# Value heads as high and low halves of one stationary tile, with a new order of the first stage, the slots and the turns

## Chip, core and metric

The kernel runs on one core of a Trainium2 chip. A core has TensorE (PE, with its weight loads shown as PEld), VectorE (DVE), ScalarE (ACT), GpSimd (POOL) and SyncE (SP, which here issues the DMAs); they run side by side, each takes its own instructions in order, and they wait for one another by semaphores. The metric is the device time of one execution in microseconds (us).

## The reference

Two layers over 512 tokens of width 1024, all in float32. Each normalises its input, projects it into the inputs of four groups of heads, mixes, gates, projects back and adds:

```python
for l in range(DEPTH):
    h = _rmsnorm(x, norm_g[l])
    p = _split(h @ w_in[l])
    o_a = _mla(...)        # latent attention, 4 heads of 64
    o_b = _diff_attn(...)  # two softmax maps per head, then an RMSNorm per head
    o_c = _dsa(...)        # the top 128 keys of a query by an index score
    o_d = _short_conv(...) # gated convolution of width 3
    y = concatenate([o_a * silu(a_gate), o_b * silu(b_gate), o_c * silu(c_gate), o_d * silu(d_gate)])
    x = x + y @ w_out[l]
return _rmsnorm(x, final_g)
```

In each attention the probabilities p of a block of 128 queries are multiplied with the values v of a head (`einsum('bhqk,bkhd->bqhd', p, v)`); a query sees the keys of its own chunk of 64 and of those before it.

## The kernel before

**Precision.** A float32 operand is split into a high part, which ACT rounds to the format that TensorE reads (`fp32r`), and a low part, what is left, which DVE or POOL subtracts (`split_w` L104, `split_ps` L113). A product is three matmuls into one PSUM bank: high x high, high x low, low x high (`mm3` L122).

**Tiling.** Tokens are four blocks of 128. Features stand on the partitions for keys and queries, tokens for values. Attention runs by pairs of heads: `pair(k)` (L422) goes through two halves of the queries (256 each), two heads and the two blocks of 128 queries of a half. For each block a unit (`unit_a`, `unit_b`, `unit_c`) computes scores and probabilities. Then the block is turned (`flip`, L410: up to four 128x128 transposes on TensorE, split into the tiles `pth` and `ptl`), and when both blocks of a head are turned, `prod` (L440) multiplies with the values into the bank `ps_o`: per block of keys three matmuls of 256 columns, of 128 for the last one. The first half of the queries sees two key blocks (a short product, 6 matmuls), the second four (a long one, 12). The value tile `vt` of a pair is 192 wide: head 0 in columns 0 to 63, zeros, head 1 in columns 128 to 191 (`vtiles`, L378; POOL writes the zeros at L384). A stationary slice of 128 columns beginning at 64 j holds head j on its own rows of the result and zeros on the other head's, so both heads add up in one 128x256 region. `post_plain` (L470) and `post_b` (its `first` is at L779) read that region once and gate it.

**Order.** Program order gives priority; a scheduler emits the order of each engine from it. The engines in `START` keep the order of the code for the first stage of layer 0. That stage is the string `FIRST[0]` (L30): `l0` loads token block 0, `s` takes its sums of squares, `n` its norm, `w` loads a piece of the first weights, `c` splits it, `e0` transposes the normalised block, and `00` is the product of block 0 with piece 0; blocks with a complete row are followed by a small norm of the latents (`first_norm`, L521). Then come seven slots (`SLOTS`, L41): slot 0 the latent projections, slots 1 to 6 one pair each (two of a, of b, of c), and with them streams of other work, interleaved by `merge` in proportion to their planned cost: `qi`, `is` (index projection and scores), `ga` to `gc` (gates), `df`, `sp` (query and key projections of b and c), `tb`, `tc` (their values), `cv` (convolution). `TOP[i]` is the planned cost of the select rounds in slot i: 48 a layer, each a MAX8 and a MATCH_REPLACE8 on DVE (L594, L595); unit_c needs their result. A unit's turn, product and gating are queued `LAG` units later.

## Time and profile before

| | us |
|---|---|
| three timed runs, median (lowest to highest) | 679.08 (679.06 to 679.42) |
| the profiled execution | 679.76 |
| its span, first to last instruction | 678.0 |
| PE, PEld busy | 622.1, 533.6 |
| DVE, ACT, POOL busy | 487.4, 364.6, 278.5 |
| select rounds of layer 0, of layer 1 | 134.2 to 219.8, 453.3 to 538 |
| first unit_c of layer 0, of layer 1 | 251.0, 573.2 |

The busy shares are means over the span. The stretches have different limits, so they are read one by one, with the chain of work that ended last inside each and the list of what an engine waited for.

### The profile page before, as it was taken

The numbers are of one execution on the slowest core, as the hardware profiler recorded it, in microseconds if no ns is written. First come the engines' busy times: TensorE is split into PE (matmuls) and PEld (weight loads), VectorE is DVE, ScalarE is ACT, GpSimd is POOL, SyncE is SP. The second block draws the span as 40 slices with busy tenths as digits, with TensorE's granted clock in tenths as the row PEclk, the third lists the DMA queues.
The fourth block names the chain that finished last, engine by engine and source line by source line (L and its number), as shares of the span: only waits on it lengthen the run. The fifth ranks groups of instructions, "written<-read, shape, count | busy, mean of one in ns | idle before, by whom it ended". The sixth has DMA issues, their size and how long they took to land.

```text
span 678.0 us, 11037 instructions
## 1 busy us (share of the span) xinstructions
PE 622.1 (92%) x3599; PEld 533.6 (79%) x3607; DVE 487.4 (72%) x1441; ACT 364.6 (54%) x879; POOL 278.5 (41%) x408
## 2 busy tenths in 40 slices
PE   1999999789999898999989899999999999999994
PEld 1877787678789677899968687879878977789994
DVE  3767762599999796645395767779999959664536
ACT  6556583484552564554364566866545256355435
POOL 2375432315434343442431854242534344344255
PEclk9999999799999999999999999999999999999998
DMA  8446573763455411233253653457244641132203
GB/s 262 117 111 191 148 133 94 185 158 99 109 145 151 118 47 43 83 125 114 58 169 91 181 171 103 139 135 170 65 115 116 190 117 48 47 109 100 80 1 125
DMA packets 86697, 80.71 MB, mean 119 GB/s; under 512 B 7302, under 2 KB 73400, under 8 KB 86640
## 3 DMA queue, kind: packets, MB, share of 16 engines
q1 hardware_dynamic: 86640, 80.02, 42.4%
q8 instruction: 28, 0.46, 0.3%
q14 instruction: 29, 0.24, 0.1%
HBM read 65.22 MB, written 12.16 MB: 114 GB/s over the span
## 4 chain that ended last, share of the span: by engine, by line
PE 58%; DVE 26%; ACT 7%; DMA 5%; issue 2%; POOL 1%; SPq 0%; ACTq 0%; DVEq 0%; POOLq 0%
PE ps_proj L127 43%; PE ps_o L127 5%; DVE ia L595 5%; DVE m L594 4%; PE ps_pt L414 3%; PE ps_s L127 2%; DMA wr<-in_w_in_dram 2%; DVE ptl L116 2%; DVE big L119 1%; DVE ps_s L490 1%; ACT prob L478 1%; DMA big<-in_x_dram 1%; PE ps_pt L302 1%; ACT prob L482 1%; DVE ia L581 1%
## 5 line engine op out<-in xcount | busy, mean ns | idle before, releaser
L101 POOL TENSOR_TENSOR wl<-wr,wh 128x256 fp32r<-128x256 f32 (+1 forms) x304 | 226.8, 779 | 326.1 <-ACT wh L106 279.4
L127 PE MATMUL ps_proj<-big,wh 128*128 128x512 f32 x768 | 250.7, 401 | 2.1 <-DVE prob L472 1.0
L127 PE MATMUL ps_proj<-wh,big 128*128 128x256 f32 (+2 forms) x768 | 173.1, 310 | 4.6 <-DVE big L116 2.1
L127 PEld LDWEIGHTS ps_proj<-big,wh 128*128 128x128 f32 x768 | 138.8, 189 | 26.8 <-issue 1.5
L127 PE MATMUL ps_proj<-big,wl 128*128 128x512 f32 x384 | 151.7, 395 | 0.0
L127 PEld LDWEIGHTS ps_proj<-wh,big 128*128 128x128 f32 x768 | 129.9, 193 | 9.6 <-DVE big L116 2.6
L127 PE MATMUL ps_proj<-wl,big 128*128 128x256 f32 (+2 forms) x384 | 116.8, 304 | 0.0
L106 ACT CAST wh<-wr 128x1024 fp32r<-128x1024 f32 (+2 forms) x84 | 83.8, 999 | 43.2 <-PE ps_proj L127 20.6
L127 PEld LDWEIGHTS ps_proj<-big,wl 128*128 128x128 f32 x384 | 72.3, 188 | 14.2
L127 PEld LDWEIGHTS ps_proj<-wl,big 128*128 128x128 f32 x384 | 74.4, 194 | 2.0
L116 DVE TENSOR_TENSOR ptl<-ps_pt,pth 128x128 fp32r<-128x128 f32 (+1 forms) x96 | 46.5, 485 | 31.4 <-ACT pth L115 30.8
L127 PE MATMUL ps_o<-pth,vt 128*128 128x256 f32 (+1 forms) x288 | 60.0, 280 | 5.2 <-ACT pth L115 3.9
L115 ACT CAST pth<-ps_pt 128x128 fp32r<-128x128 f32 (+1 forms) x96 | 40.5, 425 | 44.0 <-PE ps_pt L414 43.6
L478 ACT ACTIVATE prob<-ps_s,st_a 128x128 f32<-128x128 f32 (+1 forms) x64 | 33.8, 529 | 47.8 <-DVE st_a L490 30.7
L127 PEld LDWEIGHTS ps_o<-pth,vt 128*128 128x128 f32 x288 | 49.1, 194 | 10.0 <-ACT pth L115 6.5
L414 PE MATMUL ps_pt<-ident,prob 128*128 128x128 f32 x240 | 43.2, 278 | 10.2 <-ACT prob L482 7.1
L595 DVE MATCH_REPLACE8 ia<-m,ia 128x256 f32<-128x256 f32 (+2 forms) x96 | 52.0, 544 | 0.2
L594 DVE MAX8 m<-ia 128x8 f32<-128x256 f32 (+2 forms) x96 | 50.9, 550 | 0.1
L127 PE MATMUL ps_o<-ptl,vt 128*128 128x256 f32 (+1 forms) x144 | 42.3, 294 | 4.7 <-DVE ptl L116 4.7
L414 PEld LDWEIGHTS ps_pt<-ident,prob 128*128 128x128 f32 x240 | 28.5, 140 | 22.3 <-ACT prob L482 12.5
L482 ACT ACTIVATE prob<-prob,st_a 128x128 f32<-128x128 f32 (+1 forms) x64 | 35.8, 564 | 9.5 <-DVE st_a L481 9.3
L581 DVE SCALAR_TENSOR_TENSOR ia<-prob,widx,ia 128x256 f32<-128x256 f32 (+2 forms) x42 | 26.2, 639 | 12.7 <-ACT prob L576 12.0
(160 smaller groups left out, 949.1 us busy)
## 6 DMA issues: line engine op xcount, KB each, us to landing
wr<-in_w_in_dram SPq DMA_DIRECT2D x56, 512.0 KB
big<-trip SPq DMA_DIRECT2D x64, 128.0 KB
trip<-big SPq DMA_DIRECT2D x28, 256.0 KB
big<-in_x_dram SPq DMA_DIRECT2D x7, 512.0 KB
wr<-in_w_in_dram SPq DMA_DIRECT2D x8, 416.0 KB
big<-trip SPq DMA_DIRECT2D x32, 96.0 KB
wr<-in_w_out_dram SPq DMA_DIRECT2D x8, 384.0 KB
big<-big SPq DMA_DIRECT2D x8, 256.0 KB
```

Source lines behind the costliest of these rows:

```text
L101: nc.gpsimd.tensor_tensor(out=o[:, c], in0=a[:, c], in1=b[:, c], op=OP.subtract)
L106: nc.scalar.copy(h[:, :n], raw[:, :n])
L115: nc.scalar.copy(hi, src)
L116: nc.vector.tensor_tensor(out=lo, in0=src, in1=f(hi), op=OP.subtract)
L119: nc.vector.scalar_tensor_tensor(out=lo, in0=src, scalar=scale, in1=f(hi), op0=OP.mult, op1=OP.subtract)
L127: nc.tensor.matmul(o, lhsT=a, rhs=b, start=start and i == 0 and j == 0, stop=stop and i == n - 1 and j == 2, skip_group_check=skip)
L414: nc.tensor.transpose(b[:, k * P:(k + 1) * P], p[:, k * P:(k + 1) * P], ident)
L478: nc.scalar.activation(p[:, :W], s[:, :W], AF.Exp, scale=-1.0, bias=mn, accum_out=sums)
L482: nc.scalar.activation(p[:, :W], p[:, :W], AF.Copy, scale=st[:, 2:3])
L581: nc.vector.scalar_tensor_tensor(out=a, in0=r[:, :W], scalar=w, in1=a, op0=OP.mult, op1=OP.add)
L594: nc.vector.max(out=m8, in_=a)
L595: nc.vector.match_replace(out=a, in_to_replace=m8, in_values=a, imm_value=MARK)
```

## The change

- **Values.** A value tile is 256 wide: for each head its 64 high columns and its 64 low columns, side by side. `prod` does two matmuls per key block, with `pth` and with `ptl` as moving operand, so each gives the high and the low part at once, on the two halves of the partitions; head j goes to columns 256 j of the bank. The zero memsets are gone.
- **Joining.** A new `joined` (L476 of the changed code) copies the low half of the result on ACT to a new tile `low` (one buffer) and adds it to the high half on DVE, head by head (64x256). `post_plain` and `post_b` call it first; in `post_b` two ACT passes over the bank become one over the joined tile, and the scale `subs` moves into the last step.
- **First stage.** A new order in `FIRST[0]`; ACT, DVE and PE keep the order of the code there, as SP did. The gain of the first norm is loaded as a row of 4 KB and spread over the partitions by two matmuls with a column of ones (`gain`), instead of a 512 KB broadcast by DMA; the first square root on ACT comes ahead of everything.
- **Slots and turns.** `SLOTS`, `TOP` and `PW` are set anew; a turn is queued one unit after its scores instead of two (`LAG`), with its first transpose, and the first matmul of a product, pinned behind what PE already has.

```diff
...
 EPS = 1e-6
 BIG = 1e30
 MARK = -3e38
-FIRST = ("l0 w0 l1 l2 w1 l3 w2 w3 s0 n0 s1 c0 e0 00 n1 s2 c1 e1 01 10 11 n2 s3 e2 c2 02 12 20 21 n3 e3 c3 03 13 22 23 30 31 32 33",
+FIRST = ("l0 w0 w1 l1 w2 w3 l2 l3 s0 g0 n0 c0 e0 c1 s1 00 10 n1 e1 c2 01 11 s2 n2 20 21 c3 e2 02 12 s3 n3 22 30 31 e3 32 03 13 23 33",
          "w0 w1 c0 c1 00 10 01 11 w2 w3 c2 c3 e2 20 30 02 12 21 31 e3 03 13 22 32 23 33")
 NBIG = 20
 PIECE = 256
...
 NPROB = 7
 NGATE = 3
 NPT = 2
-NVAL = 6
-TOP = (0,0,4,16,99,0,0)
-SLOTS = ('qi ga0 bl ga1', 'is|bi df0 gb0', 'sp1 tb', 'sp0 gc0 gb1 df1', 'tc cv0', 'cv1 gc1', '')
-PW = 9.0
+NVAL = 3
+TOP = (0, 0, 4, 10, 99, 0, 0)
+SLOTS = ('qi ga0 ga1|bl', 'bi df0 gb0|is gb1', 'sp1 tb', 'sp0 gc0|df1', 'tc cv0', 'cv1 gc1', '')
+PW = 10.0
 INORDER = set()
-START = {mybir.EngineType.SP}
+START = {mybir.EngineType.SP, mybir.EngineType.Activation, mybir.EngineType.DVE, mybir.EngineType.PE}
 FM = (456, 456)
 LATE = ((3, 3),)
 FW = (("wh", "wl"), WB)
-LAG = (2,3,4)
+LAG = (1, 3, 4)
 CH = (4.0,)
 BSTEP = 2
 PL = 13.0
...
     pv = sb("val", NVAL)
     pp = sb("prob", NPROB)
     pg = sb("gate", NGATE)
+    pl_pool = sb("low", 1)
     pt_pool = sb("ptr", NPT)
     pi = sb("idx", 1)
     sm = sb("small", 4)
...
         return y
 
 
+    one = const.tile([1, P], FT, name="one")
+    grow = const.tile([1, D], FT, name="grow")
+    warm = const.tile([1, 1], FT, name="warm")
     ident = const.tile([P, P], FT, name="ident")
     make_identity(nc, ident)
     identb = const.tile([P, P], BF, name="identb")
...
         for l in range(DEPTH):
             li = 0.8 - 0.6 * math.exp(-0.3 * l)
             nc.vector.tensor_scalar(out=subs[:, l:l + 1], in0=pcol[:, l * 10 + 3:l * 10 + 4],
-                                    scalar1=1.0 - li, scalar2=None, op0=OP.mult)
+                                    scalar1=0.5 * (1.0 - li), scalar2=None, op0=OP.mult)
             pr = sm.tile([P, 2, 32], FT, name="lpr", bufs=1)
             lv = lraw[:, l, :].rearrange("p (a c b) -> p a c b", a=2, c=2)
             nc.vector.tensor_tensor(out=pr, in0=lv[:, :, 0, :], in1=lv[:, :, 1, :], op=OP.mult)
...
 
         def vtiles():
 
-            vs = []
-            for _ in range(2):
-                vs.append([pv.tile([P, NT, 192], FR, name="vt", tag="vt") for _ in range(2)])
-                for v in vs[-1]:
-                    nc.gpsimd.memset(f(v)[:, :, 64:128], 0.0)
+            vs = [pv.tile([P, NT, 256], FR, name="vt", tag="vt") for _ in range(2)]
 
             def dst(t, src):
                 sv = src.rearrange("p (a h c) -> p a h c", a=2, h=2)
                 for a in range(2):
-                    hv, lv = (v[:, t, :].rearrange("p (h c) -> p h c", c=64)[:, 0::2, :] for v in vs[a])
-                    split_ps(hv, lv, sv[:, a])
+                    w = vs[a][:, t, :].rearrange("p (h c) -> p h c", c=64)
+                    split_ps(w[:, 0::2, :], w[:, 1::2, :], sv[:, a])
             return vs, dst
 
         def gate(c0):
...
             nb = qb + 1
             b = bank("pt")
             for k in range(nb):
-                nc.tensor.transpose(b[:, k * P:(k + 1) * P], p[:, k * P:(k + 1) * P], ident)
+                i = nc.tensor.transpose(b[:, k * P:(k + 1) * P], p[:, k * P:(k + 1) * P], ident)
+                if k == 0:
+                    tc.keep_in_program_order(i)
             c = (qb % 2) * P
             split_ps(pts[0][:, :nb, c:c + P], pts[1][:, :nb, c:c + P],
                      b[:, :nb * P].rearrange("p (k c) -> p k c", k=nb))
...
                                 if j == 0:
                                     box["o"] = bank("o")
                                 o = box["o"]
-                                pts = box[j]
+                                n = 0
                                 for kb in range(nb):
                                     c = P if kb == nb - 1 else 0
-                                    mm3(o[:, c:256], [tuple(x[:, kb, j * 64:j * 64 + P] for x in v)
-                                                      + tuple(x[:, kb, c:256] for x in pts)],
-                                        start=j == 0 and kb == 0, stop=j == 1 and kb == nb - 1, skip=True)
-                                return 0.33 * nb
+                                    for x in box[j]:
+                                        n += 1
+                                        i = nc.tensor.matmul(o[:, 256 * j + c:256 * j + 256], lhsT=v[:, kb, j * P:(j + 1) * P],
+                                                             rhs=x[:, kb, c:256], start=n == 1, stop=n == 2 * nb,
+                                                             skip_group_check=True)
+                                        if n == 1:
+                                            tc.keep_in_program_order(i)
+                                return 0.22 * nb
 
                             late.append((now + LAG[1], prod))
                             if j == 1:
...
             while late and (everything or late[0][0] <= clock[0]):
                 yield late.pop(0)[1]()
 
+        def joined(o, y):
+
+            low = pl_pool.tile([64, 512], FT, name="low")
+            nc.scalar.copy(low, o[64:P])
+            for j in range(2):
+                c = slice(256 * j, 256 * j + 256)
+                nc.vector.tensor_tensor(out=y[64 * j:64 * j + 64], in0=o[0:64, c], in1=low[:, c], op=OP.add)
+
         def post_plain(box, half, y, g):
             def part():
-                nc.vector.scalar_tensor_tensor(out=y, in0=box["o"][:, :256], scalar=0.5, in1=g,
-                                               op0=OP.mult, op1=OP.mult)
+                joined(box["o"], y)
+                nc.vector.scalar_tensor_tensor(out=y, in0=y, scalar=0.5, in1=g, op0=OP.mult, op1=OP.mult)
                 return 0
             return [part]
 
...
             e4 = ep4[half]
 
             def first():
-                o = box["o"][:, :256]
                 sq = box["sq"] = prob()
-                nc.scalar.activation(sq[:, :256], o, AF.Square)
-                nc.scalar.activation(y, o, AF.Copy, scale=subs[:, l:l + 1])
+                joined(box["o"], y)
+                nc.scalar.activation(sq[:, :256], y, AF.Square)
                 return 0
 
             def second():
...
                 for i in range(2):
                     nc.tensor.transpose(b[:, i * P:(i + 1) * P], sq[:, 256 + i * P:256 + (i + 1) * P], ident)
                 nc.vector.tensor_tensor(out=y, in0=y, in1=b[:, :256], op=OP.mult)
-                nc.vector.scalar_tensor_tensor(out=y, in0=y, scalar=0.5, in1=g, op0=OP.mult, op1=OP.mult)
+                nc.vector.scalar_tensor_tensor(out=y, in0=y, scalar=subs[:, l:l + 1], in1=g, op0=OP.mult, op1=OP.mult)
                 return 0.2
             return [first, second, third]
 
...
                     first_load(int(b))
                 elif a == "c":
                     first_split(int(b))
-                elif a in "lsne":
+                elif a in "lsneg":
                     enter(int(b), a)
                 else:
                     first_part(int(a), int(b))
...
         ctx.enter_context(tc.manual_schedule(engines=INORDER))
     h = Hidden()
     x0 = {}
-    g0 = raw_tile()
-
-    warm = sm.tile([P, 1], FT, name="warm", bufs=1)
-    nc.scalar.activation(warm, ident[:, 0:1], AF.Sqrt)
+    g0 = flat(big(FT))
+
+    def gain():
+
+        for n in range(2):
+            c = slice(n * 512, (n + 1) * 512)
+            b = bank("pt")
+            nc.tensor.matmul(b, lhsT=one, rhs=grow[:, c], start=True, stop=True)
+            nc.vector.tensor_copy(g0[:, c], b)
 
     def enter(t, what, h=h):
         if what == "e":
             h.fill(t, x0[t].xn)
+        elif what == "g":
+            gain()
         elif what == "n":
             x0[t].finish()
         elif what == "s":
...
             x0[t].part(slice(512, D))
         else:
             x = flat(big(FT))
+            if t == 0:
+                nc.sync.dma_start(grow, norm_g[0:1, :])
+                nc.vector.memset(one, 1.0)
+
+                nc.scalar.activation(warm, one[:, 0:1], AF.Sqrt)
             for n in range(2 if t == 0 else 1):
                 c = slice(n * 512, (n + 1) * 512) if t == 0 else slice(0, D)
                 nc.sync.dma_start(x[:, c], x_in[t * P:(t + 1) * P, c])
-            if t == 0:
-                load_g(norm_g[0], g0)
             x0[t] = Norm(x, g0)
 
     for l in range(DEPTH):
```

On PE, a long value product of the first two pairs (`ps_o` is the bank of the results, `vt` the values, `ps_s` scores, `ps_proj` projections, `ps_pt<-ident` a transpose). Before:

```order
L728 MATMUL ps_s<-big 128x512 x3
L573 MATMUL ps_s<-kst,big 128x384
L127 MATMUL ps_o<-pth,vt 128x256
L127 MATMUL ps_o<-ptl,vt 128x256
L127 MATMUL ps_o<-pth,vt 128x256 x2
L127 MATMUL ps_o<-ptl,vt 128x256
L127 MATMUL ps_o<-pth,vt 128x256 x2
L127 MATMUL ps_o<-ptl,vt 128x256
L127 MATMUL ps_o<-pth,vt 128x256
L127 MATMUL ps_o<-pth,vt 128x128
L127 MATMUL ps_o<-ptl,vt 128x128
L127 MATMUL ps_o<-pth,vt 128x128
```

After:

```order
L414 MATMUL ps_pt<-ident,prob 128x128 x3
L742 MATMUL ps_s<-big 128x128 x3
L452 MATMUL ps_o<-pth,vt 128x256
L452 MATMUL ps_o<-ptl,vt 128x256
L452 MATMUL ps_o<-pth,vt 128x256
L452 MATMUL ps_o<-ptl,vt 128x256
L452 MATMUL ps_o<-pth,vt 128x256
L452 MATMUL ps_o<-ptl,vt 128x256
L452 MATMUL ps_o<-pth,vt 128x128
L452 MATMUL ps_o<-ptl,vt 128x128
```

Twelve matmuls became eight, alternating between `pth` and `ptl`, and the second turn of the half now stands close ahead of its product.

On DVE, the gating of the first long result and what stands around it (`ia` are the index scores that the select rounds work on). Before:

```order
L581 SCALAR_TENSOR_TENSOR ia_871<-prob,widx,ia_871 128x384
L581 SCALAR_TENSOR_TENSOR ia_872<-prob,widx,ia_872 128x512 x2
L116 TENSOR_TENSOR ptl<-ps_pt,pth 128x4x128
L116 TENSOR_TENSOR big<-ps_proj,big 128x512
L472 SCALAR_TENSOR_TENSOR prob<-ps_o,gate 128x256
L116 TENSOR_TENSOR vt<-ps_proj,vt 128x2x64
L581 SCALAR_TENSOR_TENSOR ia_870<-prob,widx,ia_870 128x256
```

After:

```order
L608 MAX m_1488<-ia_906 128x8
L595 SCALAR_TENSOR_TENSOR ia_907<-prob,widx,ia_907 128x512
L482 TENSOR_TENSOR prob<-ps_o,low 64x256
L595 SCALAR_TENSOR_TENSOR ia_907<-prob,widx,ia_907 128x512
L482 TENSOR_TENSOR prob<-ps_o,low 64x256
L117 TENSOR_TENSOR ptl<-ps_pt,pth 128x3x128
L487 SCALAR_TENSOR_TENSOR prob<-prob,gate 128x256
```

The two additions of `joined` stand ahead of the gating, and the first select round (MAX) has come before it.

On DVE, the end of the first stage: the norm of the last token block, the splits of its transposes (`big<-ps_pt`), and the latent norms (`ssa`). Before:

```order
L116 TENSOR_TENSOR big<-ps_pt,big 128x2x128 x2
L286 SCALAR_TENSOR_TENSOR big<-big,nw,wr 128x512
L116 TENSOR_TENSOR big<-ps_pt,big 128x2x128 x4
L529 TENSOR_SCALAR ssa<-ssa 128x2
L532 RECIPROCAL ssa<-ssa 128x2
L533 TENSOR_TENSOR ssa<-ssa 128x2
L534 SCALAR_TENSOR_TENSOR ssa<-ssa 128x2
L535 SCALAR_TENSOR_TENSOR ssa<-ssa 128x2
L537 TENSOR_SCALAR big<-ps_proj,ssa 128x256
```

After:

```order
L549 SCALAR_TENSOR_TENSOR ssa<-ssa 128x2
L551 TENSOR_SCALAR big<-ps_proj,ssa 128x256
L551 TENSOR_SCALAR big<-ps_proj,ssa 128x128
L543 TENSOR_SCALAR ssa<-ssa 128x2
L546 RECIPROCAL ssa<-ssa 128x2
L547 TENSOR_TENSOR ssa<-ssa 128x2
L548 SCALAR_TENSOR_TENSOR ssa<-ssa 128x2
L549 SCALAR_TENSOR_TENSOR ssa<-ssa 128x2
L551 TENSOR_SCALAR big<-ps_proj,ssa 128x256
L551 TENSOR_SCALAR big<-ps_proj,ssa 128x128
L117 TENSOR_TENSOR big<-ps_pt,big 128x2x128 x4
```

The splits of the last block's transposes, which stood ahead of the first latent norm, now stand behind two of them (the second of these and the end of the first are shown).

## Rows read from the trace of the kernel before

**Rows 1.** The page: the span, busy times, and the chain's shares by engine.
```profile
span 678.0 us, 11037 instructions
...
PE 622.1 (92%) x3599; PEld 533.6 (79%) x3607; DVE 487.4 (72%) x1441; ACT 364.6 (54%) x879; POOL 278.5 (41%) x408
...
PE 58%; DVE 26%; ACT 7%; DMA 5%; issue 2%; POOL 1%; SPq 0%; ACTq 0%; DVEq 0%; POOLq 0%
```

**Rows 2.** Busy time of each engine by stretch (begin:end, length, then engines).
```profile
core 0: us, PE busy (x) PEld busy (x) DVE busy (x) ACT busy (x) POOL busy (x), PEclk, DMA share, GB/s
41.00:134.20 93.20, 85.42 (x433) 70.67 (x433) 58.00 (x136) 52.17 (x122) 38.54 (x56) 0.96 0.59 148
134.20:219.80 85.60, 79.96 (x480) 68.99 (x479) 84.55 (x279) 45.64 (x112) 32.38 (x50) 1.00 0.52 135
219.80:251.00 31.20, 28.03 (x144) 22.09 (x143) 26.48 (x98) 16.89 (x47) 12.85 (x18) 1.00 0.31 86
251.00:349.00 98.00, 94.33 (x629) 84.49 (x631) 56.33 (x170) 49.89 (x112) 37.67 (x55) 1.00 0.27 90
...
453.30:538.00 84.70, 82.56 (x513) 72.78 (x512) 84.05 (x280) 45.44 (x113) 33.01 (x51) 1.00 0.50 129
538.00:573.00 35.00, 33.66 (x170) 26.84 (x170) 26.04 (x98) 18.15 (x49) 18.25 (x26) 1.00 0.33 88
```

**Rows 3.** The chain (start, length, work), at 58 us and around 300 us.
```profile
58.63 17.84 PE ps_proj L127 x83
...
294.61 1.37 PE ps_o L127 x12
295.97 3.28 PE ps_proj L127 x27
...
303.37 0.65 PE ps_o L127 x6
```

**Rows 4.** What PE waited for: total us, times, longest.
```profile
PE ps_pt L302 <- DVE big L286: 13.8, 1, 13.8
PE ps_pt L414 <- ACT prob L482: 7.1, 10, 1.5
PE ps_o L127 <- DVE ptl L116: 4.7, 5, 1.5
PE ps_o L127 <- ACT pth L115: 3.9, 5, 1.7
```

**Rows 5.** Groups of instructions by form: busy us, mean ns of one, idle before them.
```profile
L490 DVE CUSTOM_DVE_ANT_0 ps_s<-ps_s,bias,m 128x256 f32<-128x256 f32 x48 | 23.0, 487 | 0.5
...
L116 DVE TENSOR_TENSOR ptl<-ps_pt,pth 128x512 fp32r<-128x512 f32 x24 | 16.4, 684 | 7.3 <-ACT pth L115 7.3
...
L116 DVE TENSOR_TENSOR big<-ps_pt,big 128x256 fp32r<-128x256 f32 x32 | 12.8, 417 | 5.9 <-ACT big L115 5.6
...
L115 ACT CAST big<-ps_proj 64x512 fp32r<-64x512 f32 x16 | 9.2, 581 | 3.4 <-DVE big L116 2.1 <-PE ps_proj L127 1.1
...
L384 POOL MEMSET vt<- 128x256 f32 x24 | 6.7, 313 | 23.6 <-PE ps_o L127 23.6
...
L472 DVE SCALAR_TENSOR_TENSOR prob<-ps_o,gate 128x256 f32<-128x256 f32 x16 | 6.7, 416 | 9.4 <-PE ps_o L127 8.7 <-POOL big L101 0.7
```

**Rows 6.** DVE in order of time (start, length, work): the first block's norm factor.
```profile
7.17 0.16 DVE L283 SCALAR_TENSOR_TENSOR nw<-nw 128x1 f32<-128x1 f32 x1
```

**Rows 7.** The chain of the first 45 us, up to the latent norms.
```profile
3.09 7.95 DMA big<-in_x_dram
...
12.94 0.76 DVE big L286
13.84 1.09 PE ps_pt L302 x4
...
37.36 0.74 ACT prob L527 x4
...
41.11 0.75 DVE big L537 x2
```

## Prediction

> **What bounds the kernel now.** I read the page first [rows 1]. Over the span TensorE (PE) is busy 622.1 us of 678.0 and holds 58% of the chain that ended last; VectorE (DVE) is busy 487.4 us but holds 26% of it, so somewhere DVE is the limit. The table by stretch [rows 2] says where. While the 48 select rounds of a layer run (134.2 to 219.8, and 453.3 to 538 in the second layer), DVE works 84.55 of 85.60 us and 84.05 of 84.70. From 41.00 to 134.20 and from 219.80 on, PE is the fuller engine (85.42 of 93.20; 94.33 of 98.00) and DVE has a third or so to spare. So a microsecond of PE work is worth a microsecond outside the select windows and little inside, and DVE work the other way round.
>
> The chain in a PE stretch gives the pace of a matmul better than the busy time of one, since matmuls overlap [rows 3]: 27 projections of 256 columns take 3.28 us (0.121 each), 83 of 512 columns 17.84 us (0.215 each), a long value product (12 matmuls) 1.37 us, a short one (6) 0.65 us.
>
> Last I read what PE waits for [rows 4]: 13.8 us for its first operand, then 7.1 us before transposes of the probabilities (the "turns") and 4.7 + 3.9 us inside products, for the split of the turned block on ACT and DVE.
>
> The run of the profile took 679.76 us, 1.76 over its span and 0.68 over the median, 679.08. The sum is made against 679.76; the difference to the median is far below its uncertainty.
>
> **Value products.** Each layer has 12 long and 12 short ones. With the values' high and low halves side by side in one stationary tile, a key block needs two matmuls instead of three: 432 become 288. A third of 24 x 1.37 + 24 x 0.65 goes: 11.0 + 5.2 = **16.2 us of PE**. All of it counts where PE is the limit; inside the select windows it leaves PE idle.
>
> TensorE's price first by the row: 12 matmuls, nine of 256 and three of 128 columns, in 1.37 us. The Trainium skill ("TensorE: Matmul & The Clock Gate", Back-to-back issue gap) gives N/2.4 + 2.5 ns for an isolated matmul; an estimate by that page is 9 x 0.109 + 3 x 0.056 = 1.15 us for the same product, and 13 us saved instead of 16.2. The row is the dearer one and I stay with it.
>
> What comes in their place is on ACT and DVE. Each of the 24 results is now two halves on different partitions. `joined` copies one on ACT (64x512, nearest row 581 ns) and adds it on DVE in two pieces of 64x256 from PSUM (nearest row: 128x256, 417 ns) [rows 5]: 24 x 0.58 = 14 us of ACT, and 48 x 0.417 = **20 us of DVE** at most. Sixteen of the 24 had a DVE pass on that bank before too (416 ns) [rows 5], which now reads SBUF instead. On ACT nothing stands still for 14 us: in its fullest window it works 52.17 of 93.20 [rows 2]. On DVE the price depends on the place: by the order of the changed program 12 of a layer's 24 adds lie between its first and last select round, 12 x 0.417 = 5.0 us there; the rest falls where DVE has room. The bank of the results is held some 1.2 us longer (copy and adds against one pass); the next product into it comes several score blocks later, so I cost this at nothing, and at 24 x 1.2 = 29 us if nothing covered it. The copy waits on ACT for the product, with the exponentials of the next blocks queued behind it and the turns of those behind these; as it is queued one unit after its product (LAG 3 and 4), PE's work of a unit covers it. The 24 POOL memsets of the value tiles (313 ns, after long waits for PE [rows 5]) go; POOL is at 41% [rows 1], so they were worth nothing.
>
> **Order of the slots.** I counted instructions between markers in both orders. In layer 0, from the first stage to the first select round, 27 matmuls of 512 columns and 49 of 256 leave: 27 x 0.215 + 49 x 0.121 = 11.7 us, with the 128-column ones about 13.8. Into the select window come 46 of 512 and 31 of 256: 9.9 + 3.8 = 13.7, with the rest 15.3; between it and the first unit_c 27 and 11 leave, 7.1, with the rest 9. Layer 1 is alike: 45 of 512 enter the window, 53 leave the stretch behind it. So projections and attention units move into the windows. With them DVE work goes in: 235 instructions become 290 in layer 0's window (12 adds, 16 of the biased minimum at 487 ns [rows 5], 9 splits of the kind of 684 ns or less [rows 5], the rest small). Summed by their mean durations that is 103.6 to 122.2 us; the durations overlap (103.6 stands for 84.55 busy [rows 2]), so the window grows by 18.6 x 84.55/103.6 = 15.2 us, and in layer 1 by 15.2 x 84.05/104.8 = 12.2.
>
> Stage by stage, then: before the window of layer 0, -13.8 of PE and about -3 of its waits, -16.8; window +15.1; behind it -6.7 (between -9.2 by PE and nothing); unit_c and output -1. Layer 1: -5, +12.2, -10.5, -0.7. Moving work thus gives nearly nothing by itself; what is left is the third of the products.
>
> **First stage.** Now PE starts at 13.84. The factor of the first block's norm is ready at 7.33 [rows 6]; it is applied only at 12.94, since in DVE's order a weight split and the second block's sums stand ahead of it, and these wait for the second block of x until 11.04 [rows 7]. After the change the first block's gain needs a 4 KB row and two matmuls instead of a 512 KB broadcast, and the order is written out, so the first transposes can start at 7 to 8.5: 5 to 6 us earlier. But the order of ACT, DVE and PE is now fixed, and each PE step waits in turn for the eviction ahead of it. The largest such wait I find: the splits of the last block's transposes stand behind two whole latent norms on DVE. Such a norm took 37.36 to 41.86 here, with ACT in between [rows 7]; I count 3.7 us for PE there and 5 to 6 in smaller waits. Net -0.3, between -5 (none of these waits bites) and +2.
>
> **Turns and products.** LAG turns a block one unit after its scores instead of two, and pins a turn's first transpose and a product's first matmul behind what PE has. If the block isn't ready, all of PE stands. Measured on the order as PE work between scores and turn, and against the time that a block takes to be ready in the trace, the shortfall over all turns and products is 16.2 us after and 16.6 before. I take no change; the ends are -10 (half of the waits go) and +20.
>
> **Sum.** By stages -0.3 - 16.8 + 15.1 - 6.7 - 1 - 5 + 12.2 - 10.5 - 0.7 = -13.7. By PE alone -16.2. I take the middle, -14.8: 679.8 - 14.8 = **665.0 us**.
>
> **Rivals.**
> - A, more is gained. The first stage gives its 5 us and half of PE's waits around turns and products goes as well, since turns spread evenly: 15.7 us in rows of over 3 us, some 20 with the small entries [rows 4], so 10, of which the sum has 3 already: 665 - 5 - 7 = 653. For it: PE's first wait is 13.8 us [rows 4]; against: the fixed order of e3 behind two norms.
> - B, DVE eats half. The windows are full [rows 2], and what enters them, joins included, is paid at the full durations: 18.6 + 15.2 instead of 27.3 costs 6.5 more, so 671 to 674. The joins' 48 small adds cost 20 us by the row [rows 5], of which 10 lie in windows. The Trainium skill ("VectorE: DVE Perf Modes", Rules for kernel authors) says to keep the number of operations low, because each one drains the pipeline; that speaks against two adds where one of 512 columns would do. By the rows the second add costs 2 x 417 - 684 = 0.15 us a join, under 4 us in all.
> - C, slower. The pinned turns make PE stand: of the 48 turns and the products that follow at a short distance about 35 get a wait like the longest shown, 1.5 us, where now ten turns wait 7.1 us and ten times in products 8.6 [rows 4]. 35 x 1.5 = 52 against 16: 36 - 15 = +21, 700; it decides from 15 us of added waits, 10 turns more at full price, and with half of it the time is 683.
> - D, the change doesn't do what it says: the two matmuls cost as three did, for instance because the second waits for the low half. Then only DVE's added work shows: 680 to 685. Against it: the low half was the second operand before too, and it waited 4.7 us in all.
>
> **How the numbers follow.** Forecast (658 to 669) 0.47, A 0.23, B 0.20, C 0.07, D 0.03. A itself spreads from 648 to 657, B from 669 to 676. The range, 652 to 674, leaves out a third of A, a quarter of B and nearly all of C and D: about 0.2. 0.2% is about what a measurement here can tell from no change. Faster: all of the first three and little else, 0.88; same 0.03 (between B and D); slower 0.09.
>
> **What would show it.** Right: ps_o matmuls x288 and PE busy about 16 to 20 us lower; select windows of about 100 and 97 us, DVE full in them; the stretches ahead of and behind them shorter by 17 and 7, and by 5 and 10; the first transposes at 7 to 9 us and the first stage's end near 41. A: end near 36, and waits for turns under 4 us. B: windows over 104 us. C: waits of transposes on prob above 20 us. The forecast is wrong if PE's idle time grows by more than it does in the windows, or if the windows don't grow at all.

## The result, and the profile after

The changed kernel takes 656.86 us (median of four runs, 654.86 to 658.69) against 679.25: a ratio of 0.9667, 95% interval 0.9642 to 0.9693, or 22.4 us less. The forecast was 665.0, range 652 to 674. The profiled execution is the longest of the four (658.69, span 656.9, mean granted clock 0.982 where the others have 0.987 to 0.990), so its sums show 21 of the 22.4 us.

The page of the changed kernel, the lines that answer to [rows 1]:

```profile
span 656.9 us, 10797 instructions
...
PE 616.1 (94%) x3461; PEld 518.9 (79%) x3467; DVE 502.2 (76%) x1492; ACT 378.0 (58%) x894; POOL 270.0 (41%) x384
```

PE is busy 6 us less, not 16. Of the 10 us between, 3.8 are the gain's matmuls, which begin at 2.39 us; in the stretches below PE is busy 9.8 us less (622.1 to 612.3), with some 5 us more of them at the lower clock. The rest of the way to 16 is not accounted for. DVE and ACT each gained some 14 us of work. Busy time by stretch, cut at the same events as [rows 2] (first transposes, end of the first stage, first and last select round, first unit_c, layer 1, and the same again). The bounds here are the first MAX and the end of the last MATCH_REPLACE to the hundredth; by them the select windows before were 132.21 to 220.47 and 450.85 to 538.85, about 3 us longer than in [rows 2]:

```profile
core 0: us, PE busy (x) PEld busy (x) DVE busy (x) ACT busy (x) POOL busy (x), PEclk, DMA share, GB/s
8.52:38.51 29.99, 27.23 (x129) 21.90 (x129) 22.23 (x66) 18.56 (x56) 9.16 (x12) 1.00 0.44 134
38.51:114.63 76.12, 69.69 (x324) 56.05 (x325) 52.51 (x106) 44.77 (x101) 35.78 (x52) 0.96 0.66 164
114.63:221.58 106.95, 102.39 (x585) 86.36 (x584) 102.49 (x340) 61.50 (x153) 39.67 (x58) 0.97 0.53 136
221.58:240.61 19.03, 18.54 (x95) 14.88 (x94) 17.86 (x65) 11.52 (x26) 8.23 (x12) 1.00 0.21 61
...
431.53:534.38 102.85, 98.82 (x588) 83.88 (x587) 100.98 (x335) 60.62 (x149) 42.80 (x61) 1.00 0.51 129
534.38:553.67 19.29, 18.69 (x95) 14.91 (x94) 18.29 (x67) 11.80 (x27) 8.26 (x12) 1.00 0.24 69
```

In the windows PE and DVE are now both full (102.39 and 102.49 of 106.95). The stretches behind them, 31 and 34 us before, are 19. Cut at the same events in both profiles:

| stretch | before | after | difference | forecast |
|---|---|---|---|---|
| to the first transposes, and first stage | 41.04 | 38.51 | -2.5 | -0.3 |
| layer 0, to the first select round | 91.17 | 76.12 | -15.1 | -16.8 |
| its select window | 88.26 | 106.95 | +18.7 | +15.1 |
| to the first unit_c | 30.56 | 19.03 | -11.5 | -6.7 |
| unit_c and output | 97.93 | 95.93 | -2.0 | -1.0 |
| layer 1, to the first select round | 101.89 | 94.99 | -6.9 | -5.0 |
| its select window | 88.00 | 102.85 | +14.9 | +12.2 |
| to unit_c | 34.30 | 19.29 | -15.0 | -10.5 |
| to PE's end | 96.00 | 94.44 | -1.6 | -0.7 |

What PE waited for, as in [rows 4], the entries of 0.8 us and more at turns and products:

```profile
PE ps_pt L414 <- ACT prob L496: 5.2, 11, 1.0
PE ps_pt L414 <- DVE prob L784: 4.1, 10, 0.9
...
PE ps_o L452 <- DVE prob L482: 0.9, 2, 0.7
PE ps_pt L414 <- ACT prob L590: 0.9, 2, 0.7
PE ps_o L452 <- ACT pth L116: 0.8, 3, 0.4
```

Products, which waited 8.6 us for their turned blocks and 9.9 in all, wait 1.7 in all, of which 0.9 is for the bank `ps_o` that the joining still reads (L482). Turns wait about as long as before (10.4 for 9.9 with the small entries). And the chain through products, as in [rows 3]:

```profile
587.81 0.89 PE ps_o L452 x8
...
602.63 0.41 PE ps_o L452 x4
```

A long product takes 0.89 us instead of 1.37, a short one 0.41 instead of 0.65. Summed over all products in both traces, from the first matmul's start to the start of what follows, 53.5 us became 36.2.

### The profile page after: what moved, and what is told of

The parts are those of the page before. It is cut to its first block, busy times and chain, and to the rows that moved or that the text cites. A ratio compares the mean times of both kernels' runs of the same rounds, so it can differ in the third digit from the quotient of the medians.

```text
span 656.9 us, 10797 instructions
## 1 busy us (share of the span) xinstructions
PE 616.1 (94%) x3461; PEld 518.9 (79%) x3467; DVE 502.2 (76%) x1492; ACT 378.0 (58%) x894; POOL 270.0 (41%) x384
## 5 line engine op out<-in xcount | busy, mean ns | idle before, releaser
L102 POOL TENSOR_TENSOR wl<-wr,wh 128x256 fp32r<-128x256 f32 (+1 forms) x304 | 224.2, 770 | 314.4 <-ACT wh L107 226.7
L128 PE MATMUL ps_proj<-wh,big 128*128 128x256 f32 (+2 forms) x768 | 170.0, 307 | 4.2 <-DVE big L117 3.1
L128 PEld LDWEIGHTS ps_proj<-big,wh 128*128 128x128 f32 x768 | 141.3, 191 | 26.0 <-DVE big L120 1.4
L128 PEld LDWEIGHTS ps_proj<-wh,big 128*128 128x128 f32 x768 | 128.2, 192 | 9.2 <-DVE big L117 2.3
L128 PEld LDWEIGHTS ps_proj<-big,wl 128*128 128x128 f32 x384 | 72.8, 190 | 14.2
L492 ACT ACTIVATE prob<-ps_s,st_a 128x128 f32<-128x128 f32 (+1 forms) x64 | 33.7, 527 | 39.3 <-DVE st_a L744 19.6
L414 PE MATMUL ps_pt<-ident,prob 128*128 128x128 f32 x240 | 45.3, 288 | 11.5 <-ACT prob L496 5.2
L102 POOL TENSOR_TENSOR big<-prob,big 128x256 fp32r<-128x256 f32 x32 | 23.8, 764 | 35.9 <-ACT big L405 29.3
L452 PE MATMUL ps_o<-pth,vt 128*128 128x256 f32 (+1 forms) x144 | 35.9, 273 | 1.9 <-DVE prob L482 0.9
L452 PE MATMUL ps_o<-ptl,vt 128*128 128x256 f32 (+1 forms) x144 | 34.7, 288 | 0.0
L595 DVE SCALAR_TENSOR_TENSOR ia<-prob,widx,ia 128x256 f32<-128x256 f32 (+2 forms) x42 | 28.4, 690 | 6.8 <-ACT prob L590 5.6
```

What stands on the lines that cost most here:

```text
L102: nc.gpsimd.tensor_tensor(out=o[:, c], in0=a[:, c], in1=b[:, c], op=OP.subtract)
L128: nc.tensor.matmul(o, lhsT=a, rhs=b, start=start and i == 0 and j == 0, stop=stop and i == n - 1 and j == 2, skip_group_check=skip)
L414: i = nc.tensor.transpose(b[:, k * P:(k + 1) * P], p[:, k * P:(k + 1) * P], ident)
L452: i = nc.tensor.matmul(o[:, 256 * j + c:256 * j + 256], lhsT=v[:, kb, j * P:(j + 1) * P], rhs=x[:, kb, c:256], start=n == 1, stop=n == 2 * nb,
L492: nc.scalar.activation(p[:, :W], s[:, :W], AF.Exp, scale=-1.0, bias=mn, accum_out=sums)
L595: nc.vector.scalar_tensor_tensor(out=a, in0=r[:, :W], scalar=w, in1=a, op0=OP.mult, op1=OP.add)
```

## Experiments

An edit of this code lets the scheduler set the whole order anew, so each run gives the price of an edit with the order that follows from it. For two quantities I use sums over the ten stretches from the first transposes on: PE idle (length less PE busy), and time at the lower clock (two times one less PEclk, times the length, since the low level is half of the high one). Both come from the one profiled execution of a kernel.

**The parts by themselves.** First the products alone, in the kernel before:

```diff
-                vs.append([pv.tile([P, NT, 192], FR, name="vt", tag="vt") for _ in range(2)])
+            vs = [pv.tile([P, NT, 256], FR, name="vt", tag="vt") for _ in range(2)]
...
-                                    mm3(o[:, c:256], [tuple(x[:, kb, j * 64:j * 64 + P] for x in v)
+                                    for x in box[j]:
...
+        def joined(o, y):
```

> The kernel before with the new value products alone (value tiles of 256, two matmuls per key block, the joining on ACT and DVE, no pins); first stage, slots and turns as they were. If the third of the value products that goes from TensorE is what gained, and the 48 additions are nearly free: 679.3 - 16 = 663 (661 to 666). If the additions eat a good part of it inside the select windows, which stay as they were: 668 to 672, with the windows about 5 us longer each. If the products brought nothing by themselves and the order of the slots did it: 677 or more.

Measured: 685.92, ratio to the kernel before 1.0083 (1.0052 to 1.0115). Slower, as in the third case: neither 16 us gained nor 10.

Then all but the products, that is the changed kernel with the old ones (the diff above reversed):

> The changed kernel with the old value products (three matmuls per key block, zero halves, no joining); first stage, slots, lags as changed, turns' first transposes pinned. If the products gained 16 us and the joining is free: 656.9 + 16 = 673 (670 to 675). If the joining costs about 10 us in the select windows (12 additions of 0.417 us in each, and the copies): 663 to 667, since its cost goes too. If the order alone made the gain: 657 to 660.

Measured: 674.93, ratio 0.9915 (0.9884 to 0.9946). The new order with the old products gains 4.9 us over the runs of before taken with it (679.83), and the products in the new order 18. In the old order they lose 6.1 against the same runs. The 18 hold one thing more: in this kernel the turns' first transposes are pinned, but not the first matmul of a product; what that pin is worth alone was not run.

**The slots.**

```diff
-TOP = (0, 0, 4, 10, 99, 0, 0)
-SLOTS = ('qi ga0 ga1|bl', 'bi df0 gb0|is gb1', 'sp1 tb', 'sp0 gc0|df1', 'tc cv0', 'cv1 gc1', '')
-PW = 10.0
+TOP = (0,0,4,16,99,0,0)
+SLOTS = ('qi ga0 bl ga1', 'is|bi df0 gb0', 'sp1 tb', 'sp0 gc0 gb1 df1', 'tc cv0', 'cv1 gc1', '')
+PW = 9.0
```

> The changed kernel with SLOTS, TOP and PW of before. By my stage table the moving of work into the windows is worth little by itself: 656.9 + 2 (655 to 661), the select windows back to about 90 us and the stretches behind them to about 26 to 31. If the order is what gained, because it takes away the idle time of TensorE behind the windows and the waits of the stretch before them: 664 or more.

Measured: 691.77, ratio 1.0159 (1.0131 to 1.0186): 35 us over the changed kernel, and slower than before. That is far above the first case and inside the second, which had no upper end. With `TOP` as changed and only the streams and PW old:

> The changed kernel with the old SLOTS and PW alone, TOP as changed; the kernel with all three old took 691.8. If the streams of the slots, by which the index scores end and the select rounds begin 19 us earlier, are the cause: 686 to 693. If the share of the select rounds in slot 3 (TOP) is the cause: 657 to 662.

Measured: 693.30, ratio 1.0182 (1.0142 to 1.0221), at the upper end of the first case. It is the streams (with PW), not the share of the select rounds.

Where does the time go? In the products-alone kernel PE is busy 82.85 of 95.23 us in the first select window, at a granted clock of 0.93, and the stretch behind it runs at 0.86:

```profile
133.72:228.95 95.23, 82.85 (x470) 71.13 (x469) 91.00 (x292) 49.28 (x118) 34.57 (x50) 0.93 0.52 130
228.95:264.57 35.62, 29.42 (x132) 23.20 (x131) 26.20 (x98) 16.61 (x47) 10.81 (x16) 0.86 0.24 67
```

One stall in it is 8.10 us long. Its place in three timelines, PE, DVE and ACT:

```profile
179.70 1.22 PE L128 MATMUL ps_proj<-big,wh 128*128 128x512 f32 x2 [8.10 <-ACT prob L485]
```

```profile
174.12 1.16 DVE L601 MAX8 m<-ia 128x8 f32<-128x384 f32 x2
...
178.08 0.68 DVE L601 MAX8 m<-ia 128x8 f32<-128x512 f32 x1
178.79 0.30 DVE L497 CUSTOM_DVE_ANT_0 ps_s<-ps_s,bias 128x128 f32<-128x128 f32 x1
```

```profile
179.19 0.37 ACT L485 ACTIVATE prob<-ps_s,st_b 128x128 f32<-128x128 f32 x1 [6.32 <-DVE st_b L497]
```

PE's scores of a block (`ps_s`) were done at 171.6. The biased minimum that the block needs next, L497, stands in DVE's order behind select rounds and comes at 178.79; ACT's exponential waits for it, and PE for that. Nothing else had been put ahead on PE. The clock falls during the stall, by stretches of 5 us:

```profile
165.00:170.00 5.00, 4.88 (x23) 3.71 (x22) 4.90 (x14) 3.48 (x8) 5.00 (x7) 1.00 0.42 112
170.00:175.00 5.00, 1.49 (x9) 0.87 (x7) 4.84 (x11) 1.16 (x2) 2.82 (x5) 0.99 0.85 235
175.00:180.00 5.00, 0.30 (x1) 0.30 (x2) 4.97 (x19) 0.81 (x5) 0.00 (x0) 0.50 0.11 24
180.00:185.00 5.00, 5.00 (x14) 3.83 (x14) 4.13 (x17) 2.13 (x6) 2.81 (x4) 0.50 0.02 3
185.00:190.00 5.00, 5.00 (x24) 4.18 (x23) 4.13 (x16) 2.35 (x7) 0.00 (x0) 0.98 0.94 203
```

PE, full again from 180 on, issues 14 matmuls in 5 us at 0.50 where it issues 24 in the next 5. The four kernels with new products in old streams all have this stall, of 7.95 to 8.60 us, at 168 to 175 us; those with the new streams, or with the old products, have none above 3.9 from the first transposes on. Why the old products in the old streams escape it is not shown.

| kernel | us, median | us, profiled | PE busy | PE idle | at the lower clock |
|---|---|---|---|---|---|
| before | 679.25 | 679.76 | 622.1 | 33.2 | 10.6 |
| products alone | 685.92 | 685.22 | 613.0 | 46.8 | 33.9 |
| changed, slots old | 691.77 | 690.31 | 619.8 | 51.4 | 38.0 |
| changed | 656.86 | 658.69 | 612.3 | 27.3 | 15.8 |

Between the last two the profiled executions differ by 31.6 us (the medians by 34.9): 24.1 us of idle time and 7.5 more of busy time for the same work. The 22.2 us more at the lower clock can make up to half of themselves, 11.1, of busy time; PE stood idle in part of them.

**One stream.** The index scores (`is`) must end before the select rounds begin. In the new streams the gate projection gb1 is chained behind them, which doubles the planned cost of that stream, so that `merge` runs the scores in the first half of the slot; and gb1 no longer stands in slot 4. This one move in the products-alone kernel:

```diff
-SLOTS = ('qi ga0 bl ga1', 'is|bi df0 gb0', 'sp1 tb', 'sp0 gc0 gb1 df1', 'tc cv0', 'cv1 gc1', '')
+SLOTS = ('qi ga0 bl ga1', 'is gb1|bi df0 gb0', 'sp1 tb', 'sp0 gc0 df1', 'tc cv0', 'cv1 gc1', '')
```

> The kernel before with the new value products (values_only, 685.9) and one move of a stream: the gate projection gb1 goes from slot 4, inside the select window, into the stream of the index scores in slot 1, so that the scores end in the first half of that slot and the select rounds can begin earlier. Everything else is as before. If the begin of the select rounds is what the streams changed: the first MAX near 115 to 120, and 665 to 672. If it takes the other streams, the pins or the first stage as well: 680 or more.

Measured: 662.68, ratio 0.9747 (0.9730 to 0.9764), below the better case. From 685.92: 23 us for one name in a string, and 17 under the kernel before. The window, again with the stretch behind it:

```profile
119.86:215.13 95.27, 92.06 (x557) 80.56 (x556) 94.09 (x304) 54.33 (x129) 38.87 (x56) 1.00 0.55 146
215.13:248.20 33.07, 29.45 (x143) 23.57 (x142) 29.06 (x103) 17.48 (x48) 11.96 (x16) 0.95 0.23 68
```

It is as long as in the products-alone kernel (95.27 and 95.23) and DVE is about as full, but it holds 557 matmuls instead of 470, begins 14 us earlier, and PE keeps its clock in it. Over the whole kernel PE is idle 31.0 us and 9.7 us at the lower clock. The move does two things at once, it lets the select rounds begin earlier and takes gb1 out of slot 4, and no run separates them. And the same move undone in the changed kernel:

```diff
-SLOTS = ('qi ga0 ga1|bl', 'bi df0 gb0|is gb1', 'sp1 tb', 'sp0 gc0|df1', 'tc cv0', 'cv1 gc1', '')
+SLOTS = ('qi ga0 ga1|bl', 'bi df0 gb0|is', 'sp1 tb', 'sp0 gc0|df1 gb1', 'tc cv0', 'cv1 gc1', '')
```

> The changed kernel with that one move undone: the index scores alone in their stream, gb1 behind df1 in slot 4. If the begin of the select rounds decides: the first MAX near 133, TensorE idle some 20 us more and longer at the low clock, 680 to 693. If the move is a small part of the new streams: 657 to 664.

Measured: 673.52, ratio 0.9930 (0.9903 to 0.9957): 16.7 us worse, idle 39.3, lower clock 20.6; the first MAX comes at 125.76. That lies between the two cases that I had written down, and about half of what the old streams cost in all (36 us); which of the other streams, or PW, holds the rest was not tried.

**The joining.** The additions left out, in the products-alone kernel and in the changed one (the low part of the values is missing from the output):

```diff
-            low = pl_pool.tile([64, 512], FT, name="low")
-            nc.scalar.copy(low, o[64:P])
             for j in range(2):
                 c = slice(256 * j, 256 * j + 256)
-                nc.vector.tensor_tensor(out=y[64 * j:64 * j + 64], in0=o[0:64, c], in1=low[:, c], op=OP.add)
+                nc.scalar.copy(y[64 * j:64 * j + 64], o[0:64, c])
```

> The kernel with the new value products alone, and in it the joining without its additions: ACT copies the high half of each head's result and the low half is left out, so the output lacks the low part of the values. Takes 48 additions, about 20 us, from DVE, and leaves TensorE's work and the order of the slots as in values_only (685.9). If the additions in the full select windows are what ate the products' gain: 665 to 670, the windows back to 88. If the loss comes from the old slots and from where the scheduler puts the select rounds, whatever the additions cost: 680 or more.

Measured: 684.27, ratio 1.0050 (1.0026 to 1.0075), with the same long stall (7.95 us). The additions are not what ate the gain in the old order.

> The changed kernel with the joining without its additions in the same way (the low part of the values is left out). Its select windows are full on DVE (102.5 of 107 us) and hold about half of the 48 additions. If DVE sets the windows: 10 us less, 647 (644 to 650). If TensorE, which works 102.4 of 107 us in them too, is as much the bound: 653 to 656.

Measured: 653.92, ratio 0.9610 (0.9574 to 0.9645) against 0.9667 for the changed kernel: about 3 us for 48 additions of this size, with ACT's copies 3.3 us dearer than in the changed kernel (48 of 361 ns for 24 of 583):

```profile
L482 DVE TENSOR_TENSOR prob<-ps_o,low 64x256 f32<-64x256 f32 x48 | 19.9, 414 | 6.2 <-ACT low L479 5.7
...
L479 ACT COPY low<-ps_o 64x512 f32<-64x512 f32 x24 | 14.0, 583 | 5.6 <-PE ps_o L452 5.1
```

The first window without them is 12.6 us shorter (94.32), the stretch behind it 7.3 longer (26.30): work of PE that the window no longer covers comes out behind it.

**Turns.**

```diff
-LAG = (1, 3, 4)
+LAG = (2, 3, 4)
```

> The changed kernel with turns two units after their scores instead of one, still pinned. By the shortfalls on the order nothing changes: 656.9 (654 to 659). If turning early was worth its place, because products then find their blocks ready: 661 or more. If turning early makes TensorE wait for probabilities (9.3 us of such waits in the profile): 650 to 653.

Measured: 656.83, ratio 0.9655 (0.9618 to 0.9693). No difference in time, though the turns' waits are nearly gone, 2.2 us for 10.4. One entry of them is left above 0.8 us:

```profile
PE ps_pt L414 <- DVE prob L784: 1.6, 2, 1.2
```

PE's idle time over the stretches is 30.8 us, against 27.3: what the turns no longer wait for, other work waits for. Without the pins:

```diff
-                if k == 0:
-                    tc.keep_in_program_order(i)
...
-                                        if n == 1:
-                                            tc.keep_in_program_order(i)
```

> The changed kernel without pins on the turns' first transpose and the products' first matmul. Turns wait 9.3 us in all in the changed kernel. If the pins hold TensorE up: 650 to 654. If they are what makes products find their blocks ready (1.9 us of waits before products now, 8.6 before): 660 to 668. If neither: 656 to 658.

Measured: 665.65, ratio 0.9792 (0.9776 to 0.9808): the pins are worth 8.8 us. Its waits at the same places:

```profile
PE ps_pt L414 <- DVE prob L780: 6.6, 15, 1.1
PE ps_pt L414 <- ACT prob L492: 4.6, 11, 1.2
...
PE ps_o L450 <- DVE ptl L117: 2.7, 4, 0.9
```

Here products wait for `ptl` again, and turns too wait somewhat longer. These entries are only 2 to 4 us more; PE's idle time is 33.3 us instead of 27.3, so without the pins PE also waits elsewhere. Of the 6 us, 2.6 lie ahead of the first select window and 1.4 ahead of the second; which waits they are is not shown.

**The first stage.**

```diff
-FIRST = ("l0 w0 w1 l1 w2 w3 l2 l3 s0 g0 n0 c0 e0 c1 s1 00 10 n1 e1 ...
+FIRST = ("l0 w0 l1 l2 w1 l3 w2 w3 s0 n0 s1 c0 e0 00 n1 s2 c1 e1 01 ...
...
-START = {mybir.EngineType.SP, mybir.EngineType.Activation, mybir.EngineType.DVE, mybir.EngineType.PE}
+START = {mybir.EngineType.SP}
...
-    g0 = flat(big(FT))
+    g0 = raw_tile()
```

> The changed kernel with the first stage of before (its order, the broadcast of the gain by DMA, only SP's order fixed). In the profiles the first stage ended at 41.04 before and 38.51 after: +2.5, so 659.4 (657 to 662), with the first transposes at 13.8 and the stage's end at 41. A rival: the earlier start is taken back by the next wait (the weights' DMA or the latent norms), so that no difference is left: 656 to 658.

Measured: 658.61 (657.46 to 662.03), ratio 0.9681 (0.9646 to 0.9717), which the intervals don't tell from the changed kernel. In its profile the stage ends at 41.22 against 38.51, 2.7 us later; the timed medians differ by 1.75, the profiled executions by 0.6, so how much of it reaches the time is open. In the changed kernel PE's start and its wait at the last block's transposes:

```profile
8.52 2.16 PE L306 MATMUL ps_pt<-ident,big 128*128 128x128 f32 x8 [2.38 <-DVE big L290]
...
32.07 0.47 PE L128 MATMUL ps_s<-wh,big 128*128 128x456 f32 x1 [0.26 <-ACT big L116]
...
33.69 0.68 PE L128 MATMUL ps_s<-wh,big 128*128 128x456 f32 x2 [0.95 <-DVE big L117]
```

**A version meant to be better.** It moves the plain gating to POOL (the factor 0.5 goes into the joining, not shown) and takes the last block's transposes ahead of the second latent norm:

```diff
-                nc.vector.scalar_tensor_tensor(out=y, in0=y, scalar=0.5, in1=g, op0=OP.mult, op1=OP.mult)
+                nc.gpsimd.tensor_tensor(out=y, in0=y, in1=g, op=OP.mult)
...
-s3 n3 22 30 31 e3 32
+s3 n3 22 30 e3 31 32
```

> A version meant to beat both: the gating of the 16 plain results goes from DVE to POOL (the factor 0.5 into the joining), and the last block's transposes in the first stage go ahead of the second latent norm. Takes 16 x 0.416 = 6.7 us from DVE, of which about half in the windows, and some 1 us of waits from the first stage; without the 48 additions (20 us of DVE) the time fell by 2.9, so 0.5 to 1 us for this part by the same ratio: 655.3 (654 to 656.5). If POOL's slower pass delays what waits for the gated results: 657 to 659.

Measured: 657.84 (654.85 to 659.32), ratio 0.9672 (0.9650 to 0.9694): the same as the changed kernel. The first stage does end 1.8 us earlier (36.74), and the first window is 4.1 shorter (102.85 for 106.95), but the stretch behind it is 2.3 longer, and in layer 1 the stretch ahead of the window and unit_c are longer by 1.4 and 2.4. The changed kernel's own runs spread over 3.8 us, so what is left of such a gain can't be seen.

## Why the prediction was right, point by point

- **Value products, -16.2 us of PE: the size was right.** By the chain a long product went from 1.37 to 0.89 and a short one from 0.65 to 0.41: 24 x (0.48 + 0.24) = 17.3, and the sum over all products fell by the same 17.3. Inside products a matmul of 256 columns takes 120 ns from start to start at the median in both traces and one of 128 about 61. An estimate by the formula of the Trainium skill for an isolated matmul ("TensorE: Matmul & The Clock Gate", Back-to-back issue gap) is 109 and 56 ns; the rows decide, and they are the dearer ones. PE's busy time was the wrong sign to look for: it fell by 6 us on the page, where I had put 16 to 20, and by 14.2 in the stretches against the kernel with the old products in the new order (626.5).
- **"All of it counts where PE is the limit": right in the new order, wrong as a statement on the products.** In the old streams the same products made the kernel 6.1 us slower. The step that I missed is that work taken from PE must leave PE something to do while DVE sits in select rounds. In the changed kernel it does (102.39 of 106.95).
- **"Moving work gives nearly nothing by itself": right by itself, and the wrong question.** With old products the whole new order gains 4.9 us. With new ones the streams and PW decide over 36 us, 17 to 23 of them through one projection; with it moved, the select rounds begin earlier. I priced the move as work times pace and had no term for PE standing, nor for the lower clock that comes with it: between the old slots and the new 24 us of idle time and 7.5 of busy time.
- **The stages.** Seven of nine came within 3.6 us, and all signs are right. The mis-sized terms are the stretches behind the windows (-26.5 for -17.2): I took them between PE's work and nothing, and they followed PE's work (27.39 to 18.54 us busy in the first) and lost their idle time too (3.2 to 0.5 us). The windows grew by 33.5 for 27.3, the first with 6.4 us at the lower clock in it, so these two errors, -9.3 and +6.2 us, partly cancel, which is luck.
- **Joining, up to 20 us of DVE.** Duration right (414 ns for 417, 583 for 581); the price is 3 us, since PE is nearly as full in the windows, and its work comes out behind them. So rival B, DVE eating half, fell by its price, though one of its signs came: the first window is over 104 us (106.95), the second is not (102.85). The bank held longer, which I cost at nothing, made products wait 0.9 us. Whether one addition a join would be cheaper than two, as the rule beside B has it, no run shows.
- **Turns and products, 0 between -10 and +20.** LAG alone: 0, as taken. The pins, which I had only as a risk (rival C), are worth 8.8 us. That products then find their blocks ready, 1.7 us of waits for 9.9 in all, I had read as "no change" from the shortfalls.
- **First stage, -0.3.** It ends 2.5 us earlier in the profile; with the old one the time is 1.75 longer, which the intervals leave open. I counted 3.7 us of waiting at the last block's transposes; PE waited 0.26 + 0.95 there, because the norms ahead were already running while PE did other matmuls. The start was right (8.52, forecast 7 to 8.5).
- **Which case it was.** 656.86 lies below the forecast case (658 to 669) and within rival A (648 to 657), at its upper end. A's reasons were half right: waits before products fell by 8.2 us, of turns none, and the first stage gave at most half of its 5. Its own signs did not come (stage end 38.51 for 36, waits for turns 10.4 for under 4). Its price for turns was wrong as well: with LAG old 8 us of those waits went, and the time stayed.
- **The sum.** The middle of -13.7 and -16.2 is -15.0, not -14.8, which changes nothing. But a middle of two sums is no mechanism, and the terms that mattered most are in neither: the pins at 8.8 us, and an order of the streams that with new products is worth 36 us. That the time came into the range is in part luck.

## What to carry to other kernels

Before taking work from one engine, look at what it will do while the other one is full: in a stretch that DVE bounds, a PE that runs out of work can pay twice, with the wait and with the lower clock. Time such a change together with the order it needs, not part by part: here the parts gave +6.1 and -4.9 us, and both together -22.4. In an order that a planner emits, look for a long run of independent operations (here select rounds) ahead of the one operation that another engine waits for.

## What the runs showed of the hardware

During a stall of 8.10 us of PE, TensorE's clock fell to its low level and stayed there behind it: 0.50 in the stretches 175 to 180 and 180 to 185, with 14 matmuls in 5 us of full work where 24 went in the next 5 at 0.98. Over the kernels in the table, those with the long stall spend 34 to 38 us at the lower clock, the others 10 to 16. The Trainium skill ("TensorE: Matmul & The Clock Gate", What's actually happening) says that a gate sets the array's clock by how busy PE has been; the rows agree, with PE busy 1.49 and 0.30 of 5.00 us as the clock fell and 5.00 of 5.00 before it rose.

So long a stall is not needed. In the changed kernel the clock is 0.57 from 100 to 105 us, behind a wait of 2.33 us:

```profile
100.47 0.64 PE L587 MATMUL ps_s<-kst,big 128*128 128x256 f32 x2 [2.33 <-DVE ptl L117]
```

The changed kernel's four runs spread over 3.8 us, those of the kernel before beside them over 0.5, though over 6.5 in a later comparison. The granted clock goes with it: 0.982 in the changed kernel's longest run (658.69) and 0.990 in its shortest (654.86), 0.978 and 0.991 in those of the kernel before (683.83 and 677.36). So the time at the lower clock differs between runs of one kernel. In the profiled run of the changed kernel 6.4 us of it lie in the first window; where it lies in the other runs is not shown.
